# Differential attention in a diffusion trunk layer: weighted values two blocks back, turned weights one block back, both behind the projection unit

## The chip, the cores and the metric

The kernel runs on one NeuronCore of a Trainium2 chip. The metric is device time in microseconds (us) of one execution; the kernel before takes 1806.98 us, the median of 3 runs. Engines are named as in the profile: PE is TensorE (PEld its weight loads), DVE VectorE, ACT ScalarE, SP the queue that issues most of the DMAs.

## The reference, cut to what matters

One layer of a trunk: an FFN, a token mixer (differential attention beside an mLSTM, with a common input projection), an FFN. There are 512 latent tokens and 128 context tokens. The attention, for 8 heads with two score maps of 64 features each:

```python
def block(qi):
    s = jnp.einsum('bqhcd,bkhcd->bhcqk', qi.astype(jnp.float32), kf) * scale
    pr = jax.nn.softmax(s, axis=-1)
    w = pr[:, :, 0] - lam * pr[:, :, 1]
    return jnp.einsum('bhqk,bkhv->bqhv', w, vf)
...
out = lax.map(block, qb)
```

Latent queries (4 blocks of 128) see 768 keys: 512 latent ones and 256 of a cache. Context queries (one block) see the 128 context keys.

## The kernel before, in words

The program is one long list of instructions for each engine. PE's list is in the order in which the Python code calls `mm` (L74) and `tr` (L77); of the other engines, what stands under `written()` (L69) keeps its order among itself, and the rest is placed by the compiler's scheduler. All five engines work through their lists in order, and wait at an instruction whose operands or buffers aren't ready.

The change lies in the attention stage, 680 to 1062 us of the span. A loop over 8 heads (L2103) and, in each, over 5 query blocks `qi` (L2106) writes out, for one block:

- `scores(qi)` (L1708): 8 matmuls of float32r operands (4 for block 4, the context queries) into the PSUM tile `sc`, of which there is one only (three banks), so that the next block's scores wait until this block's are read. DVE then takes the minimum `mn` (L1728).
- `soft(qi)` (L1731): two exponentials on ACT, `p0` and `p1`, with the row sums `sm`.
- `mix(qi)` (L1739): on DVE, `rc`, `r`, and `p0 <- p1 * r + p0`, the difference of the two maps.
- `turn(qi)` (L1747): six float32 transposes on PE (four into one PSUM tile `ps_wT`, two into a second) and two ACT copies into the SBUF tile `wT`, 512 and 256 columns. Block 4 has one transpose and one copy.
- `values(qi)` (L1759): six float32 matmuls of `wT` with the values `v_tok` into `ps_o`, two rows of the trace each, and a DVE product with `rc` into `ao` (L1767). Block 4 has one matmul.

Between these stand **units** (`fill.units`, L1340): pieces of later projections, float32r products that need nothing of the attention, put there for PE to work on while DVE and ACT do the softmax. In heads 1 to 5 a unit is half of the sum for 512 output columns (12 matmuls, `wide_units`, L1360); both halves go into the one PSUM bank of `ps2w` (L2063), and after the second half ACT copies the bank out in two pieces (`k_tok`/`q_tok` or `v_tok`/`stage`). In head 0 a unit is 24 matmuls of 256 columns into a tile `ps_t`, in heads 6 and 7 it is 24 of 320 columns into `ps_p`; these take turns in the four banks of `ps2m` (L2064) with `ps_wT`, `ps_o` and the transposes `ps_qkT` of the next head's queries and keys. How many units a block has stands in `UNITS` (L2099): a pair is what comes before `mix` and what comes after `values`, so blocks 0 and 2 have 1 and 1, blocks 1, 3 and 4 have 1 and 0 (head 0: block 1 has 1 and 1; head 7: block 4 has none).

In the order before, a block is: scores of this block, turn of the last one, soft, unit, mix, values of the last one, and in blocks 0 and 2 a second unit. After block 4 come `turn(4)`, the transposes of the next head's queries (`queries`, L1689), a unit, `values(4)`. At the end of block 3 the next head's queries and keys are packed (`pack`, L1660: ACT makes `qpk` and `kpk`), and every few blocks ACT and DVE split a weight tile for coming units (`wH` on ACT, `wL` on DVE).

Of the kernel before, what the change touches and what calls it, by code (L numbers as in the profile page):

```python
# [7 lines left out]
F32 = mybir.dt.float32  # L8
# [23 lines left out]
def tile_trunk(ctx: ExitStack, tc: tile.TileContext, a: dict):  # L32
# [4 lines left out]
    def placed(ins):  # L37
        if as_written[0] is in_row:
            i = ins.ins
            if i.engine in in_row:  # L40
                tc.add_manual_dep(
                    i, in_row[i.engine].name, mybir.DependencyInfo(mybir.DependencyClass.NoSync, mybir.DependencyReason.DATA),
                    reason="written",
                )
            in_row[i.engine] = i
        elif as_written[0]:
            tc.keep_in_program_order(ins)
        return ins
# [19 lines left out]
    @contextmanager  # L68
    def written():  # L69
        was, as_written[0] = as_written[0], in_row  # L70
        yield
        as_written[0] = was

    def mm(*args, **kw):  # L74
        tc.keep_in_program_order(nc.tensor.matmul(*args, **kw))  # L75
# [1578 lines left out]
    class Head:  # L1654
# [53 lines left out]
        def scores(self, qi):  # L1708
            s = ps_s.tile([128, 1536], F32, tag="sc", name="sc")
            qs = slice(qi * 128, (qi + 1) * 128)  # L1710
            qT, kH, kL = self.qT, self.kH, self.kL
            for c in range(2):
                if qi < 4:
                    for k0, k1 in (((0, 512), (512, 768)) if c == 0 else ((0, 256), (256, 768))):
                        o = s[:, c * 768 + k0 : c * 768 + k1]
                        mm(o, qT[:, c, qs], kH[:, c, k0:k1], start=True, stop=False)
                        mm(o, qT[:, c, qs], kL[:, c, k0:k1], start=False, stop=True)
                else:

                    o = s[:, c * 512 : c * 512 + 256].rearrange("p (c t) -> p c t", c=2)  # L1720
                    mm(o, qT[:, c, qs], kH[:, :, 768:896], start=True, stop=False)
                    mm(o, qT[:, c, qs], kL[:, :, 768:896], start=False, stop=True)
            if qi < 4:
                sv = s.rearrange("p (c t) -> p c t", c=2)
            else:
                sv = s[:, 0:1280].rearrange("p (c t) -> p c t", c=2)[:, :, 0:128]
            mn, sm, rc = (ap.tile([128, 2], F32, tag=n, name=n, bufs=2) for n in ("mn", "sm", "rc"))
            placed(vec.tensor_reduce(out=mn, in_=sv, axis=AX.X, op=ALU.min))  # L1728
            self.s[qi] = sv, 768 if qi < 4 else 128, mn, sm, rc

# [68 lines left out]
    def begin_pools():  # L1799
        gates.close()  # L1800
        late_p.append(late_of.enter_context(tc.tile_pool(name="late", bufs=1, reuse_waits="tile")))
        fill.spare = late_p[0]
# [262 lines left out]
    ap = att.enter_context(tc.tile_pool(name="att", bufs=1, reuse_waits="tile"))  # L2065
# [37 lines left out]
    for hd in range(8):  # L2103
        H = heads[hd]
        odd = hd % 2
        for qi in range(5):  # L2106
            n = UNITS[hd][qi]
            with written():
                H.scores(qi)
                if qi > 0:  # L2110
                    H.turn(qi - 1)
                H.soft(qi)
            aside(hd, qi, 0)
            fill.units(n[0])
            with written():
                H.mix(qi)
            if late is not None:
                late()
                late = None
            if qi > 0:  # L2120
                with written():
                    H.values(qi - 1)
            if qi == 3 and hd < 7:
                while odd and rotate():
                    pass
                with written():
                    heads[hd + 1].pack()
            aside(hd, qi, 1)
            if (hd, qi) == (0, 2):
                begin_pools()  # L2130
            elif (hd, qi) == (6, 2):
                begin_memory()
            fill.units(n[1])
            if n[1]:
                rotate()
            with written():
                fill.ahead()
        n = UNITS[hd][-1]
        with written():
            H.turn(4)  # L2140
        if hd < 7:
            N = heads[hd + 1]
            N.queries()
            fill.units(n[0])
            with written():
                H.values(4)
            H.finish_norm()
            N.keys(0)
            fill.units(n[1])
            N.keys(1)  # L2150
            with written():
                fill.ahead()
            fill.units(n[2])
            late = H.finish
        else:
            fill.eager = True
            fill.units(1)
            H.values(4)
            H.finish_norm()
            fill.drain(3)  # L2160
            with written():
                H.finish()
# [543 lines left out]
```

## Time and profile before

| | |
|---|---|
| median of 3 runs | 1806.98 us (1805.9 to 1808.43) |
| the profiled execution's own time | 1804.37 us |
| its span in the profile | 1802.4 us |
| attention stage | 680 to 1062 us of the span |
| granted TensorE clock | 1.0 |
| PE, PEld, DVE, ACT busy | 1778.2, 1712.3, 1349.6, 899.0 us |

A row of the timeline gives the start in us from the start of the span, how long it took, the engine, the line of the kernel, the operation, out<-in by tile names, shapes, a count if several like it were merged, and in brackets how long the engine stood idle before it and who released it. Most matmuls and transposes carry L75 or L78, the lines of the two helpers, so it is the tile that tells them apart. Matmuls are pipelined: the start of a row against the start of the next one is PE's pace, while the duration reaches into the next rows.

### The profile page before, as it was taken

What the parts mean: (1) busy time and instruction counts of PE and PEld (TensorE: products, weight loads), DVE (VectorE), ACT (ScalarE), POOL (GpSimd) and SP (SyncE); (2) the same over time, 40 slices, a digit from 0 to 9 for tenths busy, and PEclk for the clock granted to TensorE, in tenths of its full rate; (3) what the DMA queues carried; (4) which work ended last, traced back from release to release, by engine and by line L of the source; (5) the groups of instructions that cost most, each with busy time, mean ns of one, the idle gap of its engine ahead of it and who ended that gap; (6) DMA issues with size and microseconds to landing.
All of it is one profiled execution on the core that took longest, in us unless ns stands there. A gap on an engine that the chain in (4) does not pass through costs nothing.

```text
span 1802.4 us, 29657 instructions
## 1 busy us (share of the span) xinstructions
PE 1778.2 (99%) x11950; PEld 1712.3 (95%) x11950; DVE 1349.6 (75%) x2162; ACT 899.0 (50%) x1579; POOL 40.8 (2%) x72
## 2 busy tenths in 40 slices
PE   8999999999999999999999999999999999999998
PEld 6999999999999999888889998899999999999998
DVE  6879887576888858777775637876768888896485
ACT  5654544332655556565655546562326545544432
POOL 0000000100000000000000000000000000000010
PEclk9999999999999999999999999999999999999999
DMA  8364565978235543222222335665642455557992
GB/s 330 110 199 162 193 241 205 360 220 279 90 120 194 187 147 96 78 72 75 72 87 98 111 121 196 201 245 190 227 164 77 143 167 190 207 176 274 355 311 82
DMA packets 144923, 317.85 MB, mean 176 GB/s; under 512 B 10577, under 2 KB 106577, under 8 KB 133009
## 3 DMA queue, kind: packets, MB, share of 16 engines
q1 hardware_dynamic: 133410, 270.20, 43.7%
q0 software_dynamic: 10688, 43.13, 7.4%
q10 hardware_dynamic: 688, 2.63, 0.4%
q8 instruction: 94, 1.54, 0.3%
q14 instruction: 43, 0.35, 0.1%
HBM read 243.77 MB, written 72.15 MB: 175 GB/s over the span
## 4 chain that ended last, share of the span: by engine, by line
PE 85%; DVE 7%; DMA 4%; ACT 2%; issue 1%; SPq 0%; ACTq 0%; DVEq 0%
PE ps_f L75 48%; PE ps_p L75 15%; PE ps_t L75 10%; PE sc L75 3%; PE ps_o L75 2%; PE ps_n L75 2%; DVE ww L54 2%; DMA raw_a<-in_w_ada_k 1%; PE ps_wT L78 1%; PE ps_u L75 1%; PE ps_qkT L78 1%; DMA raw<-in_w2b 1%; DVE junk L814 1%; DMA a_raw<-aT_dram 1%; DMA P<-nm_dram 1%
## 5 line engine op out<-in xcount | busy, mean ns | idle before, releaser
L75 PE MATMUL ps_f<-S,ww 128*128 128x320 f32 x2400 | 387.2, 309 | 4.4 <-ACT u L51 1.9
L75 PEld LDWEIGHTS ps_f<-S,ww 128*128 128x128 f32 x2400 | 359.7, 188 | 8.7 <-DVE ww L54 4.6
L54 DVE TENSOR_TENSOR ww<-raw,ww 128x2048 fp32r<-128x2048 f32 (+1 forms) x73 | 163.9, 2245 | 66.0 <-ACT ww L51 65.9
L75 PE MATMUL ps_f<-hm,ww 128*128 128x320 f32 x1176 | 185.7, 309 | 0.1
L75 PEld LDWEIGHTS ps_f<-hm,ww 128*128 128x128 f32 x1176 | 175.7, 188 | 0.4 <-DVE ww L54 0.3
L51 ACT ACTIVATE ww<-raw 128x2048 fp32r<-128x2048 f32 (+1 forms) x73 | 136.8, 1875 | 59.7 <-DVE raw L54 40.3
L54 DVE TENSOR_TENSOR raw<-raw 128x1024 f32<-128x1024 f32 x186 | 160.8, 864 | 2.4
L75 PE MATMUL ps_f<-hm,wB 128*128 128x320 f32 x1008 | 161.5, 309 | 0.0
L75 PE MATMUL ps_t<-wH,hH 128*128 128x256 f32 (+1 forms) x440 | 151.6, 345 | 1.0 <-DVE x L57 0.9
L75 PE MATMUL ps_p<-hH,wH 128*128 128x320 f32 x480 | 150.9, 314 | 1.6 <-DVE num L54 1.6
L75 PEld LDWEIGHTS ps_f<-hm,wB 128*128 128x128 f32 x1008 | 151.3, 188 | 0.0
L75 PE MATMUL ps_p<-hH,wL 128*128 128x320 f32 x480 | 148.3, 309 | 0.0
L75 PE MATMUL ps_p<-hL,wH 128*128 128x320 f32 x480 | 148.3, 309 | 0.0
L75 PE MATMUL ps_t<-wH,hL 128*128 128x256 f32 (+1 forms) x440 | 146.4, 333 | 0.9 <-DVE hL L54 0.9
L75 PE MATMUL ps_t<-wL,hH 128*128 128x256 f32 (+1 forms) x440 | 146.3, 333 | 0.0
L51 ACT ACTIVATE u<-ps_f 128x320 f32<-128x320 f32 x129 | 55.7, 432 | 154.6 <-PE ps_f L75 154.5
L54 DVE TENSOR_TENSOR wL<-raw,wH 128x2048 fp32r<-128x2048 f32 x37 | 84.6, 2288 | 25.9 <-ACT wH L51 25.9
L51 ACT ACTIVATE wH<-raw 128x2048 fp32r<-128x2048 f32 (+1 forms) x45 | 75.4, 1681 | 49.7 <-PE ps_p L75 40.3
L54 DVE TENSOR_TENSOR wB<-raw,wB 128x1024 fp32r<-128x1024 f32 x64 | 78.0, 1219 | 26.6 <-ACT wB L51 26.6
L814 DVE CUSTOM_DVE_ANT_0 junk<-raw_a,csil 128x1024 bf16<-128x1024 f32 (+1 forms) x76 | 92.6, 1218 | 2.1 <-DMA raw_a<-in_w_ada_c 1.6
L75 PEld LDWEIGHTS ps_t<-wH,hL 128*128 128x128 f32 x440 | 83.6, 190 | 9.8 <-DVE hL L54 1.1
L75 PEld LDWEIGHTS ps_t<-wH,hH 128*128 128x128 f32 x440 | 83.5, 190 | 9.4 <-ACT nsq L51 1.1
(311 smaller groups left out, 3569.7 us busy)
## 6 DMA issues: line engine op xcount, KB each, us to landing
g_dram<-g SPq DMA_DIRECT2D x44, 640.0 KB, 7.5
raw_a<-in_w_ada_c POOLq DMA_DIRECT2D x38, 512.0 KB, 5.1
g_dram<-g SPq DMA_DIRECT2D x24, 480.0 KB, 8.6
raw<-in_w1b SPq DMA_DIRECT2D x11, 1024.0 KB, 4.9
raw<-in_w3b SPq DMA_DIRECT2D x11, 1024.0 KB, 6.4
raw<-in_w1a SPq DMA_DIRECT2D x10, 1024.0 KB, 4.9
raw<-in_w3a SPq DMA_DIRECT2D x10, 1024.0 KB, 6.2
hm<-g_dram SPq DMA_DIRECT2D x7, 1280.0 KB, 13.3
```

The lines of the kernel that those rows point to most:

```text
L51: return placed(nc.scalar.activation(*args, **kw))
L54: return placed(eng.tensor_tensor(out=out, in0=in0, in1=in1, op=op))
L75: tc.keep_in_program_order(nc.tensor.matmul(*args, **kw))
L78: tc.keep_in_program_order(nc.tensor.transpose(*args, **kw))
L814: placed(vec.tensor_tensor_reduce(out=junk, in0=raw, in1=self.csil[:, v, :], op0=ALU.mult, op1=ALU.add, scale=1.0, scalar=0.0, accum_out=m ...
```

## The change

`turn` and `values` move. In a block there now come: scores of this block, soft, unit, mix, then `values` of two blocks ago, directly followed by `turn` of one block ago. After block 4, `values(3)` and `turn(4)` follow. So the float32 work of PE, transposes and weighted values, stands in one piece behind the block's first unit, where before the transposes stood ahead of the unit and the values behind it. Since `rc` of a block is now read a block later, it has three buffers instead of two.

```diff
-            mn, sm, rc = (ap.tile([128, 2], F32, tag=n, name=n, bufs=2) for n in ("mn", "sm", "rc"))
+            mn, sm, rc = (ap.tile([128, 2], F32, tag=n, name=n, bufs=2 + (n == "rc")) for n in ("mn", "sm", "rc"))
...
             n = UNITS[hd][qi]
             with written():
                 H.scores(qi)
-                if qi > 0:
-                    H.turn(qi - 1)
                 H.soft(qi)
             aside(hd, qi, 0)
             fill.units(n[0])
...
-            if qi > 0:
-                with written():
-                    H.values(qi - 1)
+            with written():
+                if qi > 1:
+                    H.values(qi - 2)
+                if qi > 0:
+                    H.turn(qi - 1)
...
         n = UNITS[hd][-1]
         with written():
+            H.values(3)
             H.turn(4)
```

The rows of PE around block 1 of head 3, before the change. `sc` are the scores (the first row is the last of block 1's, the last row the first of block 2's), `ps_wT` the turning of block 0's weights, `ps_t` the unit, `ps_o` block 0's values:

```order
L75 MATMUL sc_8667<-kL_8467,qT_8465 128x512
L78 MATMUL ps_wT_8681<-ident_4647,p0_8607 128x128 x4
L78 MATMUL ps_wT_8687<-ident_4647,p0_8607 128x128 x2
L75 MATMUL ps_t_8696<-wH_8199,hH_4471 128x512
...
L75 MATMUL ps_o_8713<-v_tok_7385,wT_8680 128x128 x6
L75 MATMUL sc_8722<-kH_8466,qT_8465 128x512
```

And the same place now. The unit follows the scores, the turning of block 0's weights follows the unit, and block 0's values have left the block:

```order
L75 MATMUL sc_8667<-kL_8467,qT_8465 128x512
L75 MATMUL ps_t_8685<-wH_8199,hH_4471 128x512
...
L75 MATMUL ps_t_8685<-wH_8199,hL_4472 128x512
L78 MATMUL ps_wT_8703<-ident_4647,p0_8607 128x128 x4
L78 MATMUL ps_wT_8709<-ident_4647,p0_8607 128x128 x2
L75 MATMUL sc_8714<-kH_8466,qT_8465 128x512
```

What stood between two blocks' scores was a turning, a unit and values; it is now a unit and a turning, twelve float32 rows of the trace less.

The end of head 3 on PE, before. `sc` are the scores of block 4, `p0_8815` the mixed weights of block 3, `p0_8871` those of block 4, and `ps_qkT` turns head 4's queries:

```order
L75 MATMUL sc_8851<-kL_8467,qT_8465 128x256
L78 MATMUL ps_wT_8861<-ident_4647,p0_8815 128x128 x4
L78 MATMUL ps_wT_8867<-ident_4647,p0_8815 128x128 x2
L75 MATMUL ps_t_8875<-wH_8199,hH_4471 128x512
...
L75 MATMUL ps_o_8892<-v_tok_7385,wT_8860 128x128 x6
L78 MATMUL ps_wT_8901<-ident_4647,p0_8871 128x128
L78 MATMUL ps_qkT_8908<-identr_4649,qpk_8845 128x128 x4
```

And now, where `ps_o_8873` are block 2's values and `p0_8796` is block 3's:

```order
L75 MATMUL sc_8843<-kL_8467,qT_8465 128x256
L75 MATMUL ps_t_8856<-wH_8199,hH_4471 128x512
...
L75 MATMUL ps_o_8873<-v_tok_7366,wT_8826 128x128 x6
L78 MATMUL ps_wT_8882<-ident_4647,p0_8796 128x128 x4
L78 MATMUL ps_wT_8888<-ident_4647,p0_8796 128x128 x2
L75 MATMUL ps_o_8892<-v_tok_7366,wT_8881 128x128 x6
L78 MATMUL ps_wT_8901<-ident_4647,p0_8852 128x128
L78 MATMUL ps_qkT_8908<-identr_4649,qpk_8837 128x128 x4
```

Block 3's weights are turned after the unit, and the values that read them (`wT_8881`) are the next thing on PE.

The end of head 7 on ACT, before. `p0_10800` is block 3's exponential, `p0_10867` block 4's; `wH` splits a weight tile:

```order
L51 ACTIVATE p0_10800,sm_10786<-sc_10776,mn_10785 128x768
L51 ACTIVATE p1_10801,sm_10786<-sc_10776,mn_10785 128x768
L51 ACTIVATE wH_10844<-raw_10487 128x2048
L51 ACTIVATE wT_10856<-ps_wT_10857 128x512
L51 ACTIVATE wT_10856<-ps_wT_10863 128x256
L51 ACTIVATE p0_10867,sm_10853<-sc_10847,mn_10852 128x128
L51 ACTIVATE p1_10868,sm_10853<-sc_10847,mn_10852 128x128
```

And now, `p0_10781` block 3's, `p0_10848` block 4's, `wT_10825` block 2's weights and `wT_10865` block 3's:

```order
L51 ACTIVATE p0_10781,sm_10778<-sc_10768,mn_10777 128x768
L51 ACTIVATE p1_10782,sm_10778<-sc_10768,mn_10777 128x768
L51 ACTIVATE wT_10825<-ps_wT_10826 128x512
L51 ACTIVATE wT_10825<-ps_wT_10832 128x256
L51 ACTIVATE wH_10836<-raw_10487 128x2048
L51 ACTIVATE p0_10848,sm_10845<-sc_10839,mn_10844 128x128
L51 ACTIVATE p1_10849,sm_10845<-sc_10839,mn_10844 128x128
L51 ACTIVATE wT_10865<-ps_wT_10866 128x512
```

The exponentials stand ahead of the copies of turned weights, where they stood behind them; here the split of a weight tile stands between.

## The prediction

> **What bounds the kernel now.** First the page: who is busy, and the chain.
>
> ```profile
> PE 1778.2 (99%) x11950; PEld 1712.3 (95%) x11950; DVE 1349.6 (75%) x2162; ACT 899.0 (50%) x1579; POOL 40.8 (2%) x72
> PE 85%; DVE 7%; DMA 4%; ACT 2%; issue 1%; SPq 0%; ACTq 0%; DVEq 0%
> ```
>
> PE is the bound: 99% busy and 85% of the chain. Then the attention stage alone, by windows (length, busy time of PE, PEld, DVE, ACT, POOL, granted clock, DMA share, GB/s):
>
> ```profile
> 680.00:1062.00 382.00, 378.63 (x2465) 342.31 (x2465) 262.02 (x401) 216.35 (x458) 0.00 (x0) 1.00 0.27 85
> ```
>
> Full clock, DVE and ACT with room. The change neither adds nor removes a matmul, so it can only move PE's waits and the price of going between float32r and float32. The waits of PE's weight loads in that stage show them better than the matmuls' (whose modelled ends cover part of a wait):
>
> ```profile
> engine line waited for: us in total, times, longest us
> PEld ps_wT L78 <- DVE p L57: 2.1, 6, 0.9
> PEld sc L75 <- ACT p L51: 1.3, 1, 1.3
> PEld ps_t L75 <- ACT stage L51: 1.0, 4, 0.3
> PEld ps_wT L78 <- PE ps_o L75: 0.8, 1, 0.8
> PEld ps_o L75 <- ACT wT L51: 0.7, 1, 0.7
> PEld ps_wT L78 <- PE sc L75: 0.6, 2, 0.4
> PEld ps_t L75 <- ACT q_tok L51: 0.5, 2, 0.3
> ```
>
> Together 7.0 us: all that PE ever waits here, and so the ceiling of what better cover can bring.
>
> **Waits that go.** Rows 1, 4 and 6 are turnings that come before their weights are mixed (4 and 6 name PE itself; but a turning needs no more than its mixed weights and a PSUM tile, so I count them in); rows 3 and 7 are units that wait for ACT to empty the wide bank. Now each turning of blocks 0 to 3 has a whole unit ahead of it, the one of block 4 a unit and more, and ACT empties the bank ahead of copying turned weights or packing. Rows 1, 3, 4, 6, 7 make 5.0 us. Of row 1, the longest 0.9 us is head 7's, whose block 4 has no unit; it is costed below, so 4.1 us go. Row 2 is in head 0's block 0, which the change doesn't touch.
>
> **Fewer changes of type.** A head has 9 float32 stretches now and 5 after (head 7: 8 and 5), 31 fewer. The price of one, from head 3's block 1:
>
> ```profile
> 834.58 0.82 PE L78 MATMUL ps_wT<-ident,p 128*128 128x128 f32 x6
> 835.21 0.50 PE L75 MATMUL ps_t<-wH,hH 128*128 128x512 f32 x1
> 835.54 0.39 PE L75 MATMUL ps_t<-wL,hH 128*128 128x512 f32 x1
> 838.06 1.50 PE L75 MATMUL ps_o<-v_tok,wT 128*128 128x128 f32 x12
> 839.31 0.47 PE L75 MATMUL sc<-kH,qT 128*128 128x512 f32 x1
> 839.62 0.39 PE L75 MATMUL sc<-kL,qT 128*128 128x512 f32 x1
> ```
>
> ```profile
> L75 PE MATMUL ps_o<-v_tok,wT 128*128 128x128 f32 x400 | 51.1, 275 | 0.5 <-ACT wT L51 0.5
> ```
>
> A unit's row goes at 0.23 us (835.54 to 838.06 are eleven); the first one after the transposes takes 0.33, so 0.1 us looks lost. But the last float32 row gives most of it back. Twelve rows of `ps_o` last 1.50 us, the last of them 0.275 (the group's mean), so their pace is 1.225 / 11 = 0.111; twelve of them and a row of `sc` should take 12 x 0.111 + 0.23 = 1.56, and 839.62 - 838.06 is 1.56. Nothing is lost behind values. Behind the six transposes, at the same pace, 0.96 (835.54 - 834.58) stand against 0.89: 0.07. Of the stretches that go, 24 end in values and 7 in a turning: 7 x 0.07 = 0.5 us, which I take, as it counts both rows at a boundary; the far end, by the first rows alone, is 31 x 0.1 = 3.1. [...]
>
> **A new wait: the next scores.** In block 1 of heads 1 to 5 no unit follows the values, so what stands between two scores loses the values. One `sc` tile means that the next scores wait for both exponentials:
>
> ```profile
> 834.78 1.76 DVE L1728 TENSOR_REDUCE mn<-sc 128x2 f32<-128x1536 f32 x1 [1.12 <-PE sc L75]
> 836.58 0.91 ACT L51 ACTIVATE p<-sc,mn 128x768 f32<-128x768 f32 x1 [0.48 <-DVE mn L1728]
> 837.47 0.90 ACT L51 ACTIVATE p<-sc,mn 128x768 f32<-128x768 f32 x1
> ```
>
> The one time that this wait binds today shows what it waits for:
>
> ```profile
> 689.82 0.89 ACT L51 ACTIVATE p<-sc,mn 128x768 f32<-128x768 f32 x1
> 690.60 0.20 ACT L51 ACTIVATION_READ_ACCUMULATOR p<-sc,mn 128x1 f32 x1
> 690.86 0.50 PE L75 MATMUL sc<-kH,qT 128*128 128x512 f32 x1 [1.07 <-ACT p L51]
> ```
>
> The first score row starts 0.15 us after the second exponential's end, so the whole tile is waited for. In head 3: the scores leave PE at 834.58, the exponentials end at 838.37, the next scores can start at 838.52. PE would be there at 834.58 + 2.75 (twelve unit rows at 0.229: 835.54 to 838.06 are eleven) + 0.63 (the turning, 835.21 - 834.58) = 837.96. Wait 0.56; today the values (1.25 us, 839.31 - 838.06) cover it. Where a `wH` or an earlier copy used to hold ACT, the copies of turned weights no longer stand ahead of the exponentials, so I take the same 0.56 in all five: 2.8 us. Were half of the tile enough it would be 0. In heads 6 and 7 the unit is 3.6 us (rows 1054.08 and 1057.69 below), and covers.
>
> In head 0, block 3, ACT's order now has the copy of that block's own unit ahead of the exponentials. They can't start before the unit's end: 2.75 + 0.1 + 0.4 (`v_tok`, below) + 1.8 (two exponentials) + 0.15 = 5.2 after the scores, and PE is there at 2.75 + 1.25 + 0.63 = 4.63: about 0.5 us.
>
> **A new wait: the end of a head.** `values(3)` now comes right behind `turn(3)`, whose copy ACT must make first. Head 7, without a unit in block 4, has that order today:
>
> ```profile
> 1048.65 1.91 ACT L51 ACTIVATE wH<-raw 128x2048 fp32r<-128x2048 f32 x1 [0.36 <-PE ps_p L75]
> 1050.40 0.82 PE L78 MATMUL ps_wT<-ident,p 128*128 128x128 f32 x6
> 1050.94 2.28 DVE L54 TENSOR_TENSOR wL<-raw,wH 128x2048 fp32r<-128x2048 f32 x1
> 1051.04 0.87 ACT L51 ACTIVATE wT<-ps_wT 128x512 f32<-128x512 f32 x2 [0.48 <-PE ps_wT L78]
> 1051.69 1.60 PE L75 MATMUL ps_o<-v_tok,wT 128*128 128x128 f32 x12 [0.47 <-ACT wT L51]
> 1054.00 0.33 PE L78 MATMUL ps_wT<-ident,p 128*128 128x128 f32 x1 [0.71 <-DVE p L57]
> 1054.08 0.39 PE L75 MATMUL ps_p<-hH,wH 128*128 128x320 f32 x1
> 1057.69 0.38 PE L75 MATMUL ps_o<-v_tok,wT 128*128 128x128 f32 x2
> ```
>
> From the first transpose to the values 1.29 us, of which the transposes take 0.63: 0.66, as the 0.7 of the waits' fifth row. Heads 1 to 6 pay it if ACT is free. Its work between two small blocks, by groups:
>
> ```profile
> L51 ACT ACTIVATE wT<-ps_wT 128x512 f32<-128x512 f32 x32 | 19.1, 597 | 52.8 <-PE ps_wT L78 52.6
> L51 ACT ACTIVATE kpk<-k_tok 128x640 fp32r<-128x640 f32 x14 | 9.5, 732 | 0.0
> L51 ACT ACTIVATE p<-sc,mn 128x128 f32<-128x128 f32 x16 | 5.9, 394 | 0.0
> L51 ACT ACTIVATE v_tok<-ps_t 128x256 f32<-128x256 f32 x15 | 5.8, 385 | 14.6 <-PE ps_t L75 14.6
> L51 ACT ACTIVATE qpk<-q_tok 128x640 fp32r<-128x640 f32 x7 | 5.1, 732 | 0.0
> L51 ACT ACTIVATE kH<-ck 128x512 fp32r<-128x512 f32 x7 | 4.5, 638 | 0.3 <-PE sc L75 0.3
> ```
>
> Counted from block 3's scores in heads 1 to 5: the turning of block 2 ends at 2.75 + 1.25 + 0.63 = 4.6, then on ACT the pair of copies 0.87, `qpk` 0.73, two `kpk` 1.46, `kH` 0.64, two exponentials 0.8: 9.1. PE: scores of block 4 (0.75), unit 2.75, values 1.25, turning 0.63: 10.0. ACT is free by 0.9 us, the wait is 0.7, 6 x 0.7 = 4.2 us. Two ends: 0 if ACT's copy were hidden, 1.6 each if one `wH` (1.91) slipped between. In head 0 a `wH` and a `v_tok` do stand there in ACT's order, behind exponentials that end at 5.05: 5.05 + 4.5 + 1.91 + 0.39 = 11.9, less about 0.9 as ACT's rows overlap by 0.1 (690.60 against 689.82 + 0.89), makes 11.0, and the first copy 0.6 more; PE comes at 5.2 + 0.75 + 2.75 + 1.25 + 0.63 = 10.6: 1.0 us. Head 7 now has `wH` ahead of the small exponentials. From block 3's scores: turning of block 2 done at 3.6 + 1.25 + 0.63 = 5.5, ACT copies to 6.3, `wH` to 8.1, exponentials to 8.9, first copy to 9.5; PE has turned block 3 at 8.0 (scores 0.55, values 1.25 from the copy's first part on, turning 0.63). The wait grows from 0.7 to some 1.6, while that for `turn(4)` falls from 0.9 to about 0.3, as `wL` (2.28, from 8.1 on) still stands ahead of that mixing: 1.9 for 1.6, 0.3 us more, between -0.9 (no `wH` in the way) and +1.5.
>
> The other queues have no new delay: SP's DMAs keep their order; DVE's `ao` products come a block later, and the banks that they free are wanted two turnings later. The third `rc` costs no time.
>
> **The sum.** Gone: 4.1 + 0.5 = 4.6. New: 2.8 + 0.5 + 4.2 + 1.0 + 0.3 = 8.8. Net +4.2 us, since PE is the bound before and after. The profiled execution took 1804.37 (span 1802.4 and 1.97 around it), so 1808.6 in its terms; it lies 2.6 under the median of the runs, 1806.98, on which I put the forecast: **1811.2 us**, slower by 0.23%. About 0.2%, 3.6 us, is what a measurement of this kernel can tell from no change.
>
> **The rivals.**
> - *Scores wait for less.* If half of `sc` were enough, or the exponentials ended sooner, the 2.8 + 0.5 go: +0.9, 1807.9, no change. Against it stands the row at 690.86. Also here: a wait at the heads' ends of half the size, +2.1, 1809.1. Chance 0.26.
> - *The stretch itself is dear* (faster). Place: the 31 stretches that go. If both the first load within one and the first behind one lay open (0.19 us each by the loads of `ps_o` and `ps_t`), 0.38 x 31 = 11.8 in place of 0.5: -7.1, 1799.9. It decides from 0.27 us a stretch on, where -4.1 - 8.3 + 8.8 = -3.6. The two sums against it are the 1.56 above and the waits' 7.0 us, which leave nothing over. [...]
>
> ```profile
> L75 PEld LDWEIGHTS ps_t<-wH,hH 128*128 128x128 f32 x295 | 55.7, 189 | 8.2 <-ACT stage L51 1.0 <-ACT q_tok L51 0.5
> L75 PEld LDWEIGHTS ps_o<-v_tok,wT 128*128 128x128 f32 x400 | 50.0, 191 | 2.7 <-ACT wT L51 0.7
> ```
>
>   Chance 0.12.
> - *ACT falls behind at every head's end*: 1.6 instead of 0.7 six times, +9.6, 1816.6. For it: strict order on ACT; against: 0.9 us in hand. Chance 0.07.
> - *It doesn't do what it says*: the printed order shows that it does; no chance.
>
> **How the numbers follow.** The forecast with the spread of its terms (+2 to +7, more room above than below) has 0.55, a quarter of it under +3.6. Slower: 0.41 + 0.07 = 0.48; same: 0.14 + 0.26 = 0.40; faster 0.12. The range goes from 1806.0, under the first rival's case, to 1815.0, which leaves out the dear stretch and the late ACT.
>
> **What the profile after would show.** Waits of `ps_wT` for `p` and of `ps_t` for `stage` and `q_tok` gone; `sc` waiting for `p` some six or seven times, 4 to 5 us with head 0's old one; `ps_o` waiting for `wT` eight times, 6 to 7 us. I'm wrong if `sc` doesn't wait in block 1, if the values at a head's end wait under 0.3 us, or if the stage gets shorter with these waits in it, which would give the stretch a price.

## The result, and the profile after

The changed kernel takes 1810.77 us (median of 7 runs, 1809.94 to 1814.23) against 1805.27 us for the kernel before (7 runs beside them, 1803.61 to 1808.43): a ratio of 1.0031, 95% interval [1.0021, 1.0041]. It is slower by 5.5 us. The profiled execution took 1812.37 us, with a span of 1810.6 us.

The page after: engines and the shares of the chain, then the attention stage by windows (same columns as before).

```profile
PE 1780.7 (98%) x11950; PEld 1713.6 (95%) x11950; DVE 1350.8 (75%) x2162; ACT 899.1 (50%) x1579; POOL 40.8 (2%) x72
PE 82%; DVE 7%; DMA 5%; ACT 4%; issue 1%; SPq 0%; ACTq 0%; DVEq 0%
```

```profile
680.00:1062.00 382.00, 373.89 (x2431) 337.27 (x2430) 262.40 (x400) 214.09 (x452) 0.00 (x0) 1.00 0.27 84
```

The work is the same: as many matmuls, the same busy times of DVE and ACT, full clock. In the stage's window PE is busy 4.7 us less (378.63 before), and ACT's share of the chain has doubled, from 2% to 4%. So PE waits for ACT. The waits of PE's weight loads in the stage, all that the view lists:

```profile
engine line waited for: us in total, times, longest us
PEld ps_o L75 <- ACT wT L51: 6.7, 9, 1.2
PEld sc L75 <- ACT p L51: 3.3, 5, 1.3
PEld ps_t L75 <- ACT q_tok L51: 1.1, 2, 0.9
PEld ps_t L75 <- ACT stage L51: 0.8, 1, 0.8
PEld ps_wT L78 <- PE ps_o L75: 0.8, 2, 0.5
```

They sum to 12.7 us, where the kernel before had 7.0: 5.7 more, and the kernel is 5.5 us slower. From the first row of `sc` to the last of `ps_o`, the stage took 375.3 us before (682.5 to 1057.8) and 380.8 now (684.7 to 1065.5), again 5.5 more. The spans differ by 8.2 us (1810.6 against 1802.4); most of the rest is the 2.2 us by which the stage began later, in a part that the change doesn't touch: the twelve kernels below, which leave that part alone too, began the stage between 680.9 and 684.3.

The largest row is the end of a head, here head 3 on PE and ACT, in order of time:

```profile
863.36 0.82 PE L78 MATMUL ps_wT<-ident,p 128*128 128x128 f32 x6
864.00 0.87 ACT L51 ACTIVATE wT<-ps_wT 128x512 f32<-128x512 f32 x2 [1.26 <-PE ps_wT L78]
864.65 1.60 PE L75 MATMUL ps_o<-v_tok,wT 128*128 128x128 f32 x12 [0.47 <-ACT wT L51]
```

ACT had been idle for 1.26 us when the first turned weights came, so it is not late; PE simply has nothing to do until the copy's first part is there. From the first transpose to the values 1.29 us pass (864.65 - 863.36), of which the six transposes need about 0.6: some 0.7 us are lost, in each of heads 1 to 6 (0.70 or 0.71 by the loads in all six).

Block 1 looks different from head to head. In head 2 the scores wait for the second exponential:

```profile
795.88 0.82 PE L78 MATMUL ps_wT<-ident,p 128*128 128x128 f32 x6
795.99 0.89 ACT L51 ACTIVATE p<-sc,mn 128x768 f32<-128x768 f32 x1
797.03 0.50 PE L75 MATMUL sc<-kH,qT 128*128 128x512 f32 x1 [0.33 <-ACT p L51]
```

In head 3 the wait is at the unit of block 1 itself, which needs the wide bank:

```profile
836.92 1.91 ACT L51 ACTIVATE wH<-raw 128x2048 fp32r<-128x2048 f32 x1
838.73 0.94 ACT L51 ACTIVATE aT<-ps_aT,gs 128x512 f32<-128x512 f32 x2
839.54 0.40 ACT L51 ACTIVATE k_tok<-ps_t 128x256 f32<-128x256 f32 x1
839.81 0.41 ACT L51 ACTIVATE q_tok<-ps_t 128x256 f32<-128x256 f32 x1
840.27 0.50 PE L75 MATMUL ps_t<-wH,hH 128*128 128x512 f32 x1 [0.42 <-ACT q_tok L51]
```

On ACT, the splitting of a weight tile and the last head's `aT` stand ahead of the two copies that empty the bank. Before, a turning (0.63 us) stood between the scores and this unit and hid it; now the unit follows the scores at once. Head 5 is like head 3. (In e_block1 below, where this turning stands there again, head 3's unit comes 0.58 us after the turning's start and does not wait.)

### The profile page after: what moved, and what is told of

It is laid out like the page before. It is cut to its first block, busy times and chain, and to the rows that moved or that the text cites. A ratio compares the mean times of both kernels' runs of the same rounds, so it can differ in the third digit from the quotient of the medians.

```text
span 1810.6 us, 29667 instructions
## 1 busy us (share of the span) xinstructions
PE 1780.7 (98%) x11950; PEld 1713.6 (95%) x11950; DVE 1350.8 (75%) x2162; ACT 899.1 (50%) x1579; POOL 40.8 (2%) x72
## 4 chain that ended last, share of the span: by engine, by line
PE 82%; DVE 7%; DMA 5%; ACT 4%; issue 1%; SPq 0%; ACTq 0%; DVEq 0%
PE ps_f L75 48%; PE ps_p L75 14%; PE ps_t L75 9%; PE sc L75 2%; PE ps_o L75 2%; PE ps_n L75 2%; DVE ww L54 2%; DMA raw_a<-in_w_ada_k 1%; DMA P<-nm_dram 1%; PE ps_u L75 1%; PE ps_qkT L78 1%; PE ps_wT L78 1%; DMA raw<-in_w2b 1%; DVE junk L814 1%; ACT p L51 1%
## 5 line engine op out<-in xcount | busy, mean ns | idle before, releaser
L51 ACT ACTIVATE p<-sc,mn 128x768 f32<-128x768 f32 (+1 forms) x80 | 62.8, 793 | 66.9 <-DVE mn L1728 66.9
```

The source lines that it names most:

```text
L51: return placed(nc.scalar.activation(*args, **kw))
```

## The experiments

Three theories. **Waits**: the stage is as long as its work plus what PE waits, and a float32 stretch costs nothing of its own. **Stretches**: entering or leaving one costs a part of a microsecond. **Waits move**: PE's waits are only the place where a lateness of ACT or DVE shows, so that mending one brings up another. The twelve kernels undo parts of the change, do parts alone, or mend single waits; two try to beat the kernel before.

First the table, to which the texts below refer. "Stretches" counts PE's unbroken float32 pieces of turnings and values in the stage's order of instructions; "waits" is the sum of the rows of PE's weight loads as above; "stage" runs from the first row of `sc` to the last of `ps_o`; the ratio is to the kernel before, beside it on the same chip.

| kernel | stretches | waits, us | stage, us | stage less waits | ratio |
|---|---|---|---|---|---|
| before | 71 | 7.0 | 375.3 | 368.3 | 1 |
| after | 40 | 12.7 | 380.8 | 368.1 | 1.0031 [1.0021, 1.0041] |
| e_tail | 40 | 13.8 | 381.5 | 367.7 | 1.0038 [1.0026, 1.0051] |
| e_block1 | 48 | 15.5 | 384.1 | 368.6 | 1.0046 [1.0034, 1.0059] |
| e_mixed | 53 | 13.5 | 381.2 | 367.7 | 1.0035 [1.0021, 1.0048] |
| e_strewn | 133 | 14.7 | 383.1 | 368.4 | 1.0045 [1.0033, 1.0058] |
| e_tail_queries | 46 | 9.7 | 378.0 | 368.3 | 1.0014 [1.0006, 1.0023] |
| e_late | 40 | 20.9 | 391.6 | 370.7 | 1.0092 [1.0078, 1.0106] |
| b_block1 | 63 | 13.8 | 380.1 | 366.3 | 1.0029 [1.0017, 1.0040] |
| b_block4 | 64 | 14.0 | 382.8 | 368.8 | 1.0040 [1.0026, 1.0054] |
| e_late2 | 40 | 12.7 | 380.8 | 368.1 | 1.0026 [1.0017, 1.0035] |
| e_both | 46 | 9.8 | 377.8 | 368.0 | 1.0016 [1.0007, 1.0025] |
| b_pack | 71 | 5.9 | 374.2 | 368.3 | 0.9993 [0.9984, 1.0002] |
| b_both | 71 | 6.8 | 375.3 | 368.5 | 0.9997 [0.9988, 1.0006] |

### e_tail: block 3's values behind the next unit

The changed kernel, in heads 1 to 6 with `values(3)` beside `values(4)`, behind the unit that follows the next head's queries.

```diff
+        under = 0 < hd < 7
         with written():
-            H.values(3)
+            if not under:
+                H.values(3)
             H.turn(4)
...
             with written():
+                if under:
+                    H.values(3)
                 H.values(4)
```

> The changed kernel, but in heads 1 to 6 values(3) stands after the next unit, beside values(4), so that nothing on PE follows turn(3) that needs its copy. If the waits make the loss: 6 x 0.73 us of waiting for wT go, 4.4 us, and of the change's +5.5 us against before about +1.1 is left (ratio 1.0006, from 1.0000 to 1.0015). If a wait that is taken away only turns up further down (next head's queries, later values): +4 to +5.5 stays. If the float32 stretches had a price of their own: no difference in their number here (40 and 40), so the same as the first.

Measured: 1810.43 us (1809.87 to 1814.32), ratio 1.0038 [1.0026, 1.0051] to 1803.77. Not faster than the changed kernel. PE's waits, the rows over 1 us:

```profile
PEld ps_aT L78 <- DVE ao L54: 4.5, 4, 1.8
PEld sc L75 <- ACT p L51: 4.5, 7, 1.3
PEld ps_o L75 <- ACT wT L51: 2.5, 3, 1.2
PEld ps_qkT L78 <- ACT wT L51: 1.2, 6, 0.2
```

The wait for `wT` fell from 6.7 to 2.5, the 4.2 us that were to go. But the last values of a head are now later, so DVE's norm of `ao` is, and the transposes `ps_aT` of that norm, which stand in the next head's block 0, wait 4.5 us for it in four heads. The scores wait 1.2 us more, in heads 3 and 5 too. Here waits move: the mend itself delayed something that PE needs some 13 us later (behind head 1 the values start at 771.86, the transposes at 785.03).

### e_block1: block 1 as before

```diff
                 H.scores(qi)
+                if qi == 1:
+                    H.turn(0)
                 H.soft(qi)
...
             with written():
+                if qi == 1:
+                    H.values(0)
+                if qi > 2:
+                    H.values(qi - 2)
                 if qi > 1:
-                    H.values(qi - 2)
-                if qi > 0:
                     H.turn(qi - 1)
```

> The changed kernel, but block 1 of every head as before: turn(0) ahead of the unit, values(0) behind it; blocks 2 to 4 as changed. If the waits make the loss: the scores' wait for the exponentials and the unit's wait for the wide bank in block 1 of heads 1 to 5 go, 0.6 + 0.6 + 0.8 + 0.6 + 0.85 = 3.4 us, and +2.1 against before is left (ratio 1.0012, from 1.0004 to 1.0020). If the waits only move: +4 to +5.5 stays. If stretches are dear (0.27 us each): 8 more of them, +2.2 on top of that.

Measured: 1813.13 us (1810.72 to 1813.65), ratio 1.0046 [1.0034, 1.0059]. Not faster than the changed kernel, where 3.4 us less was expected; the stage is 3.3 us longer, by waits that the edit opens. Of PE's waits, the rows of the scores and of the wide bank:

```profile
PEld sc L75 <- ACT p L51: 3.3, 4, 1.3
PEld ps_t L75 <- ACT stage L51: 2.2, 3, 1.6
PEld ps_t L75 <- ACT q_tok L51: 2.2, 2, 1.6
```

With block 0's values back in block 1, block 2 has only a turning (0.62 us) between its two units, and the second waits up to 1.6 us for the bank that the first has just filled; and `sc` waits in block 4 of heads 2 and 4 instead of in block 1. The values of two blocks ago were the cover between these units.

### e_mixed: heads 0 and 7 in the order before

Heads 1 to 6 have block 1 as before and block 3's values behind the next unit (both edits above); heads 0 and 7 have the order before.

```diff
+        under = 0 < hd < 7
...
+                if qi == 1 or qi > 0 and not under:
+                    H.turn(qi - 1)
...
-                if qi > 1:
-                    H.values(qi - 2)
-                if qi > 0:
+                if qi == 1 or qi > 0 and not under:
+                    H.values(qi - 1)
+                elif qi > 1:
+                    if qi > 2:
+                        H.values(qi - 2)
                     H.turn(qi - 1)
...
         with written():
-            H.values(3)
             H.turn(4)
...
             with written():
+                if under:
+                    H.values(3)
                 H.values(4)
```

> Heads 0 and 7 in the order before; in heads 1 to 6 block 1 as before, blocks 2 to 4 as changed, values(3) after the next unit. If the waits make the loss: both new waits are out and the old ones of heads 1 to 6 (turnings 1.2 us, wide bank 1.7 us) too, so 3 us faster than before (ratio 0.9983, from 0.9975 to 0.9992). If stretches are dear: 18 fewer than before at 0.27 us make 4.9 more, about 0.9956. If waits only move: 1.0000.

Measured: 1811.08 us (1808.93 to 1812.37), ratio 1.0035 [1.0021, 1.0048]. Slower, where 3 us faster was expected. It has the waits of both edits: 4.5 us at `ps_aT` as in e_tail, 2.8 at `sc`, 1.9 at the wide bank. My estimate had left out the waits that the two edits open.

### e_strewn: 93 more stretches

The changed kernel with the six value matmuls strewn one by one among the unit's products, so that the number of float32 stretches goes from 40 to 133 with the work the same.

```diff
     def mm3(ps, lh, ll, rh, rl, first, last):
...
+        if strewn:
+            strewn.pop(0)()
...
+            if qi > 1:
+                strewn.extend(H.products(qi - 2))
             fill.units(n[0])
+            while strewn:
+                strewn.pop(0)()
...
-                    H.values(qi - 2)
+                    H.weigh(qi - 2)
```

> The changed kernel, but in blocks 2 to 4 the six matmuls of values(qi - 2) are strewn one by one between the products of the unit: the same work, 133 float32 stretches in place of 40. At the 0 to 0.07 us of the rows: 0 to 6.5 us more than the change, about 2 (ratio to before about 1.004). At 0.27 us a stretch or more: 25 us more (ratio to before 1.017 and over).

Measured: 1812.47 us (1810.09 to 1813.94), ratio 1.0045 [1.0033, 1.0058]. The stage is 2.3 us longer than after (383.1 against 380.8), of which 2.0 are waits. The rest, 0.3 us for 93 stretches, is 0.003 us each; as the last column of the table scatters by about 0.6 us, it may be up to 0.01 each. One of these stretches, in head 2:

```profile
797.75 0.39 PE L75 MATMUL ps_o<-v_tok,wT 128*128 128x128 f32 x2
797.89 0.47 PE L75 MATMUL ps_t<-wH,hH 128*128 128x512 f32 x1
798.20 0.40 PE L75 MATMUL ps_t<-wL,hH 128*128 128x512 f32 x1
```

Two float32 rows at 0.111 and one of the unit at 0.23 make 0.45, and 798.20 - 797.75 is 0.45: the unit's first row takes 0.31, but the float32 rows ahead of it take that much less. The same shows across the table: from 40 to 133 stretches the stage less its waits stays between 367.7 and 368.8 us (but for two kernels, below). This settles **stretches** for those that hold values, the kind that e_strewn adds: no price that this profile can show. Those that end in a turning are read from their rows under "Why the prediction was right".

### e_tail_queries: block 3's values behind the next head's queries

Now the mend of the head's end without e_tail's delay: only the ten transposes `ps_qkT` go between, and the last values come no later.

```diff
+        under = 0 < hd < 7
         with written():
-            H.values(3)
+            if not under:
+                H.values(3)
             H.turn(4)
         if hd < 7:
             N = heads[hd + 1]
             N.queries()
+            if under:
+                with written():
+                    H.values(3)
             fill.units(n[0])
```

> The changed kernel with one thing moved: in heads 1 to 6 the values of block 3 come behind the transposes of the next head's queries, no longer right behind the turning whose copy they read. The transposes then run during ACT's copy, and, other than in the run that put these values behind the unit, the values of block 4 are no later than in the changed kernel. By the theory that the loss is what PE waits and nothing else, 0.73 us go in each of six heads, less some 0.2 each for the transposes that now wait for a PSUM bank which the copy empties: 3 us less, attention stage 377.5 to 378.5 us, ratio to the kernel before 1.0014. By the rival that a wait removed here always turns up further down, as it did behind the unit, the stage stays at 380 to 382 us, ratio 1.003 or more. By a price of the float32 stretches nothing would change (the number of stretches is the same within 6).

Measured: 1807.26 us (1805.05 to 1808.53), ratio 1.0014 [1.0006, 1.0023] to 1804.69. As **waits** had it, 1.0014, and outside what **waits move** gave. PE's waits, the largest rows:

```profile
PEld sc L75 <- ACT p L51: 3.3, 5, 1.3
PEld ps_o L75 <- ACT wT L51: 2.5, 3, 1.2
PEld ps_qkT L78 <- ACT wT L51: 1.2, 6, 0.2
...
```

4.2 us go at `ps_o`, 1.2 come at `ps_qkT`, and the other rows stand as they did. So the wait at the heads' ends is a real cost of the change, 3.0 us of waits net (2.8 in the stage), not a place where another lateness shows.

### e_late: the last head's `aT` in block 1

The norm's end (transposes on PE, their copy on ACT, a DMA) in block 1 of the next head instead of block 0.

```diff
-            if late is not None:
+            if qi == 1 and late is not None:
                 late()
```

> The changed kernel with the end of the last head's norm (its six transposes on PE, their copy on ACT) put into block 1 instead of block 0 of the next head. It tests what makes the waits of block 1: if the scores of block 2 wait because only a turning stands between unit and scores, 0.5 us more of transposes there cover it; and if the unit of heads 3 and 5 waits because ACT's copy of these transposes (0.9 us) stands ahead of its emptying of the wide bank, that wait goes too. By this theory the scores' waits of heads 1, 2 and 4 (0.47 to 0.59 us) and the bank's of heads 3 and 5 (0.67, 0.72) shrink to 0.1 to 0.2 each: 2 to 2.9 us less, attention stage 378 to 379 us, ratio 1.0017. By the rival that the waits only move (DVE or ACT being what is late), the stage stays within 1 us of 380.8, ratio 1.003.

Measured: 1820.84 us (1819.29 to 1821.46), ratio 1.0092 [1.0078, 1.0106]. Ten us slower than the changed kernel, which no theory had. One place makes it, in head 1 (SP, then PE):

```profile
748.07 0.37 SPq L97 DMA_DIRECT2D raw<-in_w_dk  x1
748.49 0.50 SPq L97 DMA_DIRECT2D raw<-in_w_dq  x1
749.09 0.45 SPq L1785 DMA_DIRECT2D aT_dram<-aT  x1
754.80 4.73 SPq L97 DMA_DIRECT2D QQ<-qq_dram  x2
757.88 1.30 PE L78 MATMUL ps_c<-ident,QQ 128*128 128x128 f32 x5 [8.39 <-DMA QQ<-qq_dram]
```

`QQ` is loaded into a buffer of the tag `asq`, which `aT` uses too. In the changed kernel `aT` leaves at 742.70 and `QQ` is asked for at 744.93; now `aT` leaves at 749.09, behind two weight loads of 512 KB, and `QQ` can start only when `aT` is out, at 754.80 (SP waits 5.2 us for that DMA, 1.8 in the changed kernel). PE stands still for 8.4 us at the transposes of `QQ`. After that the granted clock stays at a half for some 5.8 us, which explains the 2.5 us by which this kernel's stage exceeds its waits (below, in the last section).

### b_block1: one part of the change alone

The kernel before; block 0's values go to block 2, all turnings stay, and `rc` has its third buffer.

```diff
-            mn, sm, rc = (ap.tile([128, 2], F32, tag=n, name=n, bufs=2) for n in ("mn", "sm", "rc"))
+            mn, sm, rc = (ap.tile([128, 2], F32, tag=n, name=n, bufs=2 + (n == "rc")) for n in ("mn", "sm", "rc"))
...
-            if qi > 0:
+            if qi > 1:
                 with written():
+                    if qi == 2:
+                        H.values(0)
                     H.values(qi - 1)
```

> The kernel before with one part of the change alone: block 0's values are no longer in block 1 but in block 2, directly ahead of block 1's. All turnings stay where they were. In heads 1 to 5 the scores of block 2 then lose 1.25 us of cover: by the theory they wait 0.5 to 0.6 us for block 1's exponentials in each, 2.7 us in all, attention stage 378 us, ratio 1.0015. By the rival that joining float32 stretches pays (eight fewer) it comes out nearer 1.000. If the turnings' own waits for the mixed weights, which stay here, hold PE anyway, less than 1 us is added.

Measured: 1809.19 us (1806.83 to 1811.35), ratio 1.0029 [1.0017, 1.0040]; 1.0015 was expected. The scores' row is 5.9 us against 1.3 before, and the row of the turnings that wait for the mixed weights 4.7 against 2.1. Against PE's pace the scores' first rows come late by 0.45 to 0.48 us in heads 1, 3 and 5, about what was expected, and by 0.93 to 0.97 in heads 2 and 4, twice that. Head 2:

```profile
788.61 1.90 ACT L51 ACTIVATE wH<-raw 128x2048 fp32r<-128x2048 f32 x1
790.41 0.85 ACT L51 ACTIVATE wT<-ps_wT 128x512 f32<-128x512 f32 x2
791.15 0.90 ACT L51 ACTIVATE p<-sc,mn 128x768 f32<-128x768 f32 x1
793.08 0.50 PE L75 MATMUL sc<-kH,qT 128*128 128x512 f32 x1 [0.81 <-ACT p L51]
```

The `wH` and then the copy of block 0's turned weights, which the turning ahead of the unit put there, stand ahead of the exponentials; these start at 791.15, 0.5 us after the minimum was there (788.90 + 1.76, a row of DVE). In the changed kernel, where that turning comes later, head 2's scores wait less (0.33 idle against 0.81). So this part of the change costs what cover it takes away, and more where ACT is behind. (In this kernel the loads overstate PE's loss, as a load can wait while earlier matmuls still run: in head 1 the scores' load waits 0.75 us and the next turning's 0.43, but by the starts of PE's rows they come late by 0.47 and 0.17. Five such pairs would make up to 2.7 us, and 366.3 in the table falls some 2 us short of the other kernels; that this is the whole of it isn't shown.)

### b_block4: the other part alone

The kernel before; in block 4 the turning of block 3 goes behind the unit, directly ahead of its values.

```diff
-                if qi > 0:
+                if 0 < qi < 4:
                     H.turn(qi - 1)
                 H.soft(qi)
...
                 with written():
+                    if qi == 4:
+                        H.turn(3)
                     H.values(qi - 1)
```

> The kernel before with the other part alone: block 3's weights are turned behind block 4's unit, right ahead of the values that read them; blocks 0 to 3 stay as they were. By the theory the values wait 0.73 us for ACT's copy in heads 1 to 6, 4.4 us, and the old waits of these turnings for the mixing (about 1.6) go. The unit of block 4 then starts one turning earlier, and in four heads must wait up to 0.6 us for the wide bank, since on ACT the packing of the next head's keys stands there: 2.4. Together about +5 us, attention stage 379 to 381 us, ratio 1.0028. If ACT empties the bank in time, +2.8, ratio 1.0015. If joining stretches pays (seven fewer), below 1.000.

Measured: 1811.13 us (1810.52 to 1812.55), ratio 1.0040 [1.0026, 1.0054]; 1.0028 was expected.

```profile
PEld ps_o L75 <- ACT wT L51: 6.7, 8, 1.4
PEld ps_t L75 <- ACT stage L51: 3.6, 4, 1.2
PEld ps_t L75 <- ACT q_tok L51: 2.0, 3, 1.2
```

`ps_o` waits 6.7 us for `wT`, the same sum as in the changed kernel. The wide bank was undersized: 5.6 us in seven waits, four of them 1.1 to 1.2, where up to 0.6 was foreseen in each of four heads. The turning (0.6) and its own wait (0.25) had stood ahead of the unit, and with both gone the old 0.3 become 1.2. In the change the copies that empty the bank come ahead of the packing in ACT's order, here behind it: in head 3 the two pieces of packing start at 856.20 and 856.83, the copies at 858.08 and 858.35. Either part alone is about as slow as both together.

### e_late2 and e_both: the mends again

e_late with head 1 left as it was, and the same together with e_tail_queries.

```diff
-            if late is not None:
+            if late is not None and (qi == 1 or hd == 1):
                 late()
```

> The run that put the end of the last head's norm into block 1, mended: there one DMA (the head's turned values to memory) got ahead of a load of gate values on SP in head 1, that load came 10 us later, and PE stood still for 8.8 us before the transposes of what it brings. Now head 1 keeps the changed kernel's place and only heads 2 to 7 have it in block 1. Outside of that stall the mended waits were read in the first run: scores in heads 2 and 4 0.3 each for 0.57 to 0.59, the wide bank in heads 3 and 5 0.47 and 0.43 for 0.67 and 0.72, but a second wait of 0.37 for the bank in each of these blocks. By the theory that the stage's length follows the waits the sum stays about where it was: 0.3 to 0.5 us less than the changed kernel, attention stage 380.3 to 380.8 us, ratio 1.0029. If the stall of PE was not a matter of that DMA, the time stays near 1.009.

Measured: 1809.21 us (1807.66 to 1810.46), ratio 1.0026 [1.0017, 1.0035] to 1803.72: the stall is gone with head 1's edit, and the sum of waits is that of the changed kernel, 12.7 us. `sc` waits 0.5 us less, the wide bank 0.3 more. In all 0.3 to 0.5 us less was expected. Here waits move once more.

> The changed kernel with both mends: block 3's values behind the transposes of the next head's queries (heads 1 to 6), and the end of the last head's norm in block 1 (heads 2 to 7). By the theory that what counts is the sum of PE's waits: 12.6 us of waits in the changed kernel, less 2.8 for the first mend, less 0.3 to 0.5 for the second, leaves 9.3 to 9.5 for 7.1 in the kernel before: 2.3 us slower than that, ratio 1.0012, stage 377.6 to 377.8 us. By the theory that joining the float32 stretches pays something of its own it comes out below 1.0005.

Measured: 1806.68 us (1805.42 to 1811.11), ratio 1.0016 [1.0007, 1.0025], stage 377.8 us; 1.0012 and 377.6 to 377.8 were expected. With 46 stretches for 71 it is still slower than the kernel before, by about what its waits are longer (9.8 against 7.0 us).

### b_pack and b_both: towards a faster kernel

b_pack: the kernel before; in heads 1 to 6 the packing of the next head goes behind block 4's exponentials, and half of block 2's values behind block 4's scores.

```diff
                 H.scores(qi)
+                if qi == 4 and 0 < hd < 7:
+                    H.values(2, 1)
                 if qi > 0:
                     H.turn(qi - 1)
                 H.soft(qi)
+                if qi == 4 and 0 < hd < 7:
+                    heads[hd + 1].pack()
...
-                    H.values(qi - 1)
+                    H.values(qi - 1, 0 if qi == 3 and 0 < hd < 7 else None)
```

(Here `values` takes a half: 0 the first three matmuls, 1 the other three. The old call of `pack` stays for head 0 alone.)

> The kernel before with its own waits at the end of a head mended, an attempt to beat both kernels: the packing of the next head's queries and keys (2.2 us on ACT) goes behind block 4's exponentials, so that ACT empties the wide bank ahead of it; and of block 2's six value matmuls three go behind the scores of block 4, where they cover the mixing for which the turning of block 3 waits. Heads 1 to 6. In the kernel before, these two waits are 0.23 to 0.27 us in five heads and 0.29 to 0.33 in four, 2.5 us together; the scores of block 4 lose 0.63 us of cover, of which they had 0.7. By the theory 2.0 to 2.5 us go: stage 373 us, ratio 0.9987. By the rival that waits move, ACT's packing makes the transposes of the next head's queries late instead, by 0.3 to 0.8 us a head, and the ratio is 0.9995 to 1.001.

Measured: 1802.74 us (1801.74 to 1808.18), ratio 0.9993 [0.9984, 1.0002]: not to be told from the kernel before, though the profile's stage is 1.1 us shorter.

```profile
PEld ps_wT L78 <- DVE p L57: 2.1, 6, 0.9
...
PEld ps_t L75 <- ACT q_tok L51: 0.2, 1, 0.2
PEld ps_t L75 <- ACT stage L51: 0.2, 1, 0.2
```

The bank's waits fell from 1.5 to 0.4 us, as much as the stage. The turnings' waits stayed at 2.1, and the idea behind that half was wrong: moving values from ahead of the scores to behind them leaves PE's work between block 3's scores and the turning as it was, so the turning comes no later.

b_both: the packing as in b_pack, and block 3's turning behind the first three products of block 4's unit, which does put work ahead of it.

```diff
+            if qi == 4 and 0 < hd < 7:
+
+                def third():
+                    with written():
+                        H.turn(3)
+                        H.soft(4)
+                        heads[hd + 1].pack()
+
+                strewn.append(third)
             aside(hd, qi, 0)
             fill.units(n[0])
...
```

> The kernel before, mended at the end of heads 1 to 6: the packing goes behind block 4's exponentials, as in the run of the packing, and block 3's weights are turned behind the first three products of block 4's unit (0.69 us) in place of ahead of it. Moving half of block 2's values did nothing for the turning's wait for the mixed weights (0.23 to 0.28 us in five heads, still there in that run), as the work between the scores of block 3 and the turning stayed the same; three products do add work ahead of it. By the theory that the stage is as long as its work and PE's waits, 1.2 us go with the bank's waits and another 1.2 with the turnings': 4.6 to 5.3 us of waits in place of 7.1, stage 372.9 to 373.5 us, ratio 0.9987. By the rival that waits move (exponentials of block 4, copies and packing now all come 0.5 us later on ACT), the transposes of the next head's queries wait 0.3 us or more in each head, and the ratio is 0.9995 or above.

Measured: 1803.25 us (1802.50 to 1806.20), ratio 0.9997 [0.9988, 1.0006] to 1804.78, stage 375.3 us. The turnings of block 3 no longer wait, but those of block 4 do, 0.40 to 0.45 us in five heads by the loads. Head 3, DVE and PE:

```profile
857.55 0.82 DVE L54 TENSOR_TENSOR qpk<-q_tok,qpk 128x640 fp32r<-128x640 f32 x1 [2.12 <-ACT qpk L51]
858.29 0.16 DVE L1746 RECIPROCAL rc<-sm 128x2 f32<-128x2 f32 x1
859.14 0.33 PE L78 MATMUL ps_wT<-ident,p 128*128 128x128 f32 x1 [0.22 <-DVE p L57]
```

DVE's part of the packing, which waits for ACT's, stands ahead of the mixing of block 4. **Waits move** was right here. No kernel of the twelve is shown to be faster than the kernel before.

## Why the prediction was right

It forecast 1811.2 us, slower by 4.2; it is slower by 5.5, at 1810.77 us. That the times lie 0.4 us apart is partly luck: the forecast stands on 1806.98 us for the kernel before, 1.7 above the 1805.27 of the seven runs, and the change was put 1.3 too low. Step by step:

- **PE's waits are the whole effect.** Right, and the best supported reading here: over fourteen kernels the stage follows the sum of the waits, and less its waits it is 367.7 to 368.8 us (with the two exceptions named).
- **The end of a head**, 6 x 0.7 = 4.2. Right: 6.7 us in the row of `ps_o`, of which six times 0.7 are these heads'. e_tail_queries takes them away, pays 1.2 at `ps_qkT` for it, and the stage is 2.8 us shorter.
- **Head 0's end**, 1.0, and **head 7**, 0.3. Head 0's values start 0.80 us after PE's last row (1.04 by the loads). In head 7 `wH` did come ahead of the small exponentials: by the loads its values wait 1.23 us, and 0.20 at block 2's, for 0.71 before, and its last turning 0.51 for 0.90. That is 0.3 more in all. Right.
- **The next scores in block 1**, 2.8 for five heads. Right in size where it came, wrong in its place for two heads. In heads 1, 2 and 4 the scores wait, 0.43 to 0.57 us each by the loads; the row of `sc`, 3.3 us, holds these, the 0.5 foreseen for head 0's block 4, and the old 1.3. "4 to 5 us, some six or seven times" was foreseen; it is five times. In heads 3 and 5 the wait comes one step earlier, at the unit (0.85 and 0.84 by the loads), and the scores behind it don't wait.
- **Waits that go**, 4.1. This is the step that failed: rows 3 and 7 of before, the unit's waits for the wide bank, 1.5 us, were counted as gone. They went from block 4, where ACT now empties the bank ahead of the packing, but the same kind, 1.9 us, appeared in block 1 (heads 1, 3 and 5), since the turning no longer stands between scores and unit. I had looked only at what the unit does for the turning, and not at what the turning did for the unit. The turnings' own waits (rows 1, 4 and 6) did go, apart from block 4's in heads 0 (0.32, not foreseen) and 7.
- **Fewer changes of type**, 0.5 gained. Not there, and the size came from one odd place. The 0.07 us were read in head 3's block 1, where the time from the turning's start to the unit's second row is 0.96. One block on, in the same kernel, it is 0.88:

```profile
840.79 0.82 PE L78 MATMUL ps_wT<-ident,p 128*128 128x128 f32 x6
...
841.67 0.39 PE L75 MATMUL ps_t<-wL,hH 128*128 128x512 f32 x1
```

  In twelve other places of heads 1 to 5 of that kernel, where a unit that doesn't wait follows a turning, it is 0.88 to 0.91, the 0.89 that the paces give, so nothing is lost behind a turning either. The stage less its waits went from 368.3 to 368.1.
- **The rivals.** *The stretch is dear* fell with e_strewn: at 0.27 us each its stage would have been 25 us longer than that of the changed kernel, not 2.3. (The 0.38 us of its sum, two loads lying open at each stretch, was an estimate that no run shows: e_strewn leaves up to 0.01 us for a stretch that holds values. The loads of `ps_t` and `ps_o` last about the same in both kernels, 189 and 191 ns.) *Scores wait for less* fell by the rows of head 2: the scores start 0.15 us after the second exponential's end (795.99 + 0.89). *ACT falls behind at each end* fell by the 1.26 us that ACT was idle in head 3, and by the same wait of 0.70 or 0.71 in all six heads.

The 1.3 us between 4.2 and 5.5, by kinds of wait: the bank was put 1.9 too low, the scores 1.3 too high, the turnings 0.5 too low and the values 0.1 too high, 1.0 in all; the stretches make up the other 0.3 (0.5 foreseen, 0.2 seen, which the rounding of the rows could make). That the first two nearly cancel is luck. All of it is less than the interval of the measurement (the ratio's ±0.001 is 1.8 us), so the split rests on the profiles alone, one of each kernel.

## What to carry to other kernels

Where one engine is 98% busy, as here, an order is worth what that engine waits (less its waits the stage was 367.7 to 368.8 us in twelve kernels of fourteen), so price a reordering by listing for each piece what it covered for its neighbours on both sides, and check the neighbour that moves up as well as the piece that moves. Then a mend must not make anything later that the same engine needs further down: the same wait was filled with ten transposes that were due anyway, which gained 3 us (e_tail_queries), and avoided by delaying the values, which gained nothing (e_tail). A price per boundary should be read in more than one place: the 0.07 us came from the one turning of fourteen that showed it, and 93 stretches more cost nothing that can be told from zero.

## What the runs showed of the hardware

**One stall cost more than its length.** In e_late PE stood still from about 749.5 to 757.9 us, 8.4 us. The stage by windows around it (length, busy PE, PEld, DVE, ACT, POOL, granted clock, DMA share, GB/s):

```profile
752.00:754.00 2.00, 0.00 (x0) 0.00 (x0) 1.12 (x4) 1.19 (x4) 0.00 (x0) 0.85 0.94 340
754.00:756.00 2.00, 0.00 (x0) 0.00 (x0) 0.70 (x1) 0.00 (x0) 0.00 (x0) 0.50 0.18 42
...
760.00:762.00 2.00, 2.00 (x7) 1.52 (x6) 0.00 (x0) 0.00 (x0) 0.00 (x0) 0.50 0.55 164
762.00:764.00 2.00, 2.00 (x7) 1.58 (x6) 0.00 (x0) 0.00 (x0) 0.00 (x0) 0.59 0.00 0
764.00:766.00 2.00, 2.00 (x20) 2.00 (x19) 0.57 (x2) 0.79 (x3) 0.00 (x0) 1.00 0.04 8
```

The granted clock fell to a half about 3.9 us into the stall (a mean of 0.85 from 752 to 754 puts it at 753.4) and came back at about 763.6, 5.8 us after PE had work again; in between, a unit's products run at 0.43 us each:

```profile
760.26 0.63 PE L75 MATMUL ps_t<-wH,hH 128*128 128x512 f32 x1
760.69 0.63 PE L75 MATMUL ps_t<-wL,hH 128*128 128x512 f32 x1
```

for 0.23 at full clock. Some 5.8 us at half pace lose about 2.9, an estimate from these rows; the load's wait in the table (8.8 us) is 0.4 longer than PE's stall, so 2.5 us are left beside the waits. The waits of the change itself, 0.2 to 1.3 us, are far shorter, and the granted clock of its stage is 1.00.
